# Retention, heads 1 to 7: the latent tokens' projections by seven block products; y and gate in DRAM, four weight slots

## The chip, the cores and the metric

The kernel runs on one core of a Trainium2 chip. The metric is the device time of one execution in microseconds (us). Engines are named as in the profile: PE (TensorE, with its weight loads PEld), DVE (VectorE), ACT (ScalarE), POOL (GpSimd), SP (SyncE, which here only issues DMAs).

## The reference, cut to what matters

Two layers work on 512 latent tokens and 256 context tokens of width 1024, in float32. Layer 0 is neighbourhood attention beside spatial gating, layer 1 is retention; each is followed by a gated MLP with a convolution over neighbouring tokens (FFN). The change lies in layer 1:

```python
splits = [RET_QK_WIDTH, 2 * RET_QK_WIDTH, 2 * RET_QK_WIDTH + RET_V_WIDTH]   # 1024, 2048, 4096
q, k, v, g = jnp.split(h_lat @ w_in, splits, axis=-1)
q = apply_rope(q.reshape(B, T, H, dk), cos, sin)                            # H = 8, dk = 128
k = apply_rope(k.reshape(B, T, H, dk) * dk ** -0.5, cos, sin)
v = v.reshape(B, T, H, dv)                                                  # dv = 256
kc, vc = jnp.split(h_ctx @ w_in[:, RET_QK_WIDTH:2 * RET_QK_WIDTH + RET_V_WIDTH], [RET_QK_WIDTH], axis=-1)
...
for d in range(2):                                                          # forward, backward
    s_ctx = retention_final_state(rev(kc), rev(vc), lg)
    outs_lat.append(rev(retention_chunked(rev(q), rev(k), rev(v), lg, s_ctx)))
...
on = ((o - mu) * lax.rsqrt(var + EPS)).reshape(B, N, RET_V_WIDTH) * gn_g
return (jax.nn.silu(g) * on.astype(g.dtype)) @ w_out
```

The latent tokens need all four projections, the context tokens k and v only.

## The kernel before

**Numbers.** A float32 product is made of three matmuls of a rounded type. `split` makes a high part on ACT (L171) and the rest on DVE (L172); `mm3` (L215 to L218) issues high by high, high by low, low by high. The normalized, modulated tokens lie in SBUF as such a pair (`h0c`, `h1c`).

**Weights.** A unit is 128x1024 numbers. SP loads it into one of three buffers `raw` (L157), `split` writes it into a slot of the ring `w0` to `w5`, and PE reads it there. A slot is written anew when PE has used it, a buffer when both halves of the split (and whoever else reads it) are done.

**Heads.** `retention` runs eight heads. For a head from 1 on: k (`rk`) and q (`rq`) of the latent tokens, 24 matmuls of 512 columns each; rotation (`rope`, with a product on POOL, L1221); k in natural order (`kn`); v of 128 latent tokens at a time, two to a bank, and of the context tokens, and the gate, 256 columns each (`rn`, by `nat`); scores (`rs`), states (`stc`, `stl`), the products within a chunk (`ro`) and across chunks (`rx`), and the norm with the gate (`norm`, its power on POOL, L1367). The decay matrices come from ACT and POOL (L1212, L1213). Between them stands the output product of the head before (`wr`, by `out_group`): eight pieces of 128x512, which DVE adds to y in SBUF (L678). The row of the second layer's modulation is worked out beside it on DVE (`ada_half`, `acc`, L326, six background jobs). Head 0 has an order of its own and isn't changed; the last two heads' output comes in `out_last`.

**Order.** `queue` reads the table `ORDER` and chains every engine's instructions in the order written there, one list for PE, DVE, ACT, POOL and SP each. Nothing is reordered at run time: an instruction waits at the head of its queue, and all behind it wait with it.

**The FFN.** It already uses seven products of half blocks instead of eight (`px`, `py`, `pz`), with its weight sums on DVE, and adds its result to DRAM with accumulating DMAs, issued by POOL (L1734).

Of the kernel before, what the change touches and what calls it, by code (L numbers as in the profile page):

```python
# [10 lines left out]
F32 = mybir.dt.float32  # L11
F32R = mybir.dt.float32r
# [6 lines left out]
P = 128  # L19
# [32 lines left out]
c-p;Nd8{4RS^wtDnSI~x+<kxd?Yp1-{1(SsV#izD_}N+P#Ez4YCUKi4X_Is#ZBx`#Ep3Bn)0P4)sBEQz3Mx<wv>*_mB2>|Tsf0u&{s0Li{@`D}Gt  # L52
0d*cX6Ie%CYaAJ2Pj_obxTe@ArK(PX+)BbckC8n$bRh-#=2s?*@MGjDZ{0)zEWi_4p&YxNS9|21<GeE+yMdm<kKg;1FHHn!XWj=Hk6ia<||U96SM
gxYLERfTJ7&IFfcwwyOXOU;~&_5D$0i9{3c8+s|=Hk3Z)=&Xp_pLvwKOD!l9C9CZ5Er(4@Nyawbd{;D0^#BUOh4HuzeorTj$U$$VJ3^)O9%~&$Y^
gXs$hPS_|L;JJrYh^;`yOQmM^SCNW9Q?+14X)#N6+eglLBE61YPGFbfBsdF$BbhR9n7t}kjjg-dHg&EkH$N9N6SGWUKlfGyVIYPv63!T!*4Nj-{F
h0^JqlNc&nDZ;x!Il=d#i}GSvAIfCuv$Xk{&SzipDXu1`4rKWtK8CAnkg4*o)Rsx;no6MM+EEr1tcbD}YAvF(XeX7@v&$ZUr6R4qD!>ph2?U+18J
oBE^h?c}z-ak`$vB|Q9&PqQv3mYD&$*Wq*>fawyZ``woEv$%$z$0HPo&TJgIy{;Zb3sPgTFSB(y41P{#JEHS5aELB=Z}vnav-s}pg0oO(mKLA80q
|Y!J6!ILpC|FO5O*R$9ecKaYBR5RCZvzDi$4G#W`eqf=vRf8Q33#al-=|V4l#%!%0tN|XP9#&R&@D=;l=Jns9HoYdkWwtJb8QLm6O@vc9AJ(*d!0
+_I^7usKHWk>G0od_dhszlPwu%59|Nf@9-s(S@aX>O0oSu+kS%^Bb58|CcO?{WW9cceQ5~MQDdHr-hVU^-=zpPN1gVavHjuLPJ9`=3mf9uxAf_ZS
YSDsAHa4Tt|9@)&~!HO%IdM$Vg7-G&kp>}Pe%DZ2mi_?qg5m4u_~z-e33KZZ#npD4!)OmVVAx1RJ8cv`LH|7O!u|-JRcn#Mb)Fn;vwcL^RZ(?iS0  # L60
+T(zOV7!W@zhd)M|jxR350iLo`)2k0;xS%Pu6nrUvV1j8LYHIJ&SL^3^*&;)(#5ZR-+!d=+f&I8m--%L$vXTmJ*hT||XrVZMkaPW7@P|v_;2X^|k
{?A|Ih6gwoeLpZ^_?g6#(uVBet}k<MaJv)wA5B;Z{Cq-VATmBtijaCSodQk>H*8wB(kq`FiWLVMj8LtypHF9DV$h12aIijz#Wlu~97wc0A78N%Ay
cC5Z2Wz4oYr2Cr20lywx8qP|1YuZ{yr<h!^4+e0cOZ{Y+6zRc+j_=6a9JTA?x^dN~3bqDGp*Cz<0Rsa&&O+tGHV#{^?*g-{w|NXRghvt(*BB1t-Y
# [12 lines left out]
GEf5pL<xW%Xn3#`<dOlP*Ami`$x-f4co-3iXc-w*BY68rz)Qy+v^3UA$O*i3ekz?jKQSXdd99WWrAwo)c|=IqJa@X`;%M9y$q_O=)C2|e9C&hnqV
w^~SC`DCTuTmk7V+K=OY|HS13(6t;<j^ge6e!@MUsm1N9O^AeFkMH(nu3sfM2>+k$0*wuDDK@c}B6H7|5cUVL_ndm0_*wOiZF`bqJqvG(ihfp6E-
`cIw&`4c6?=p7b|#l`DsaFU;N!-DJBWNqYc+>XGGezmTpa989%v{uu_$<NU!rs4>WFFE%=zsPxxPYKq?r`)o{FB-jSt6}YEGXiXQ6Es@+IIAB0H$
QUws%Ce_#o$*SI0oJ)A?yZ*j@<Nr30Cvd2K*<<gs0``&bYNIv-^S>yXSUcK=#{Q3l!E5+@^N$XA~4gW?K-1Po)HuK)B<2?a`$L?bwJ`u@G?s@)KI
QEQsj+LwSAdcYye1=PLyp_{yCyl;?h%QGjP|!SX+<bg_nAG87zs-#}Mla7f^Vnm>b>4Sndv1<NM$BQn%2M9q$CA7L4VTM0?j8ladvb*HFpOuxQ|Y  # L80
3vWh+@9<GwXM{B%oM_hVll80=q4$wqUe$cS1v38!o)|Bxsep*(P@d52^SYHHwP)9J`hM1=ZuzpA)5NPN%atueOJ|H>@m>tx7)5&^2(uvL$?42Hzv
`I+SjmFY>1dB=zM0o&J;sUePhlpB=C;6KxytE2QFX7MYvwB+&J;M8x#N4^<V(vT{?6tkL@R1CA31>~Hok*E5R<iFm(=`VBeCda<z^ZCRl70bz3u_
WQ(?@nvL&B$oZoQ-J_!<onNmf28pdCST8=&+cwY0U#e$ai)`jPWwh4LKAm=Kg!OTC|dY?H3q<9v8t7R=kngUi5y*_qY|jzj8v1MYYQ;ovAwZ>dUW
lNvieo1QW?(%F4SY1l-|Aq7TC5VS7yBYh@pmn@k)Ha*?C|#z0b-Kb{}GGc=hkwoJ@X{w?nP&(Y?0xsfaOV0gAG`G++(;^$o~${x>xNwR=PpNv5|G
s1~sv6Q}&z3*$>ZEG|yPoQ{}zQirKG1U(!{WdU;`K*ovoJpoAmwiTY<18}<hSq(kyca%{1?{U@idl=%aA$&nygYJb^vV44SW1AHo=v3|Cl$$W*Sg
93X{Qt84%6u7^b<@soA7n^U8kmTEts&UsHy~XYG!uLk=muT!xWF0f_(fE6@1H-KJ-XSl?)e%KCPk!-+0Uh@5WWB0E(t+s$DB6IL47(q^IH>T@;kf
MPqYTqf7JE64Wd8#hF!C>hW}4?CJdS3aq!mmn`s!rU$Y}7+lo~RuL4HS9HUaM8Z@2XSqBMONfLY+-3c6(`r+8NM=m9;0Ztr6;_2L2B?B$6NMf-PD
# [51 lines left out]
class Trunk:  # L139
# [986 lines left out]
    def weigh(self, h, b, pr, hd):  # L1126
# [46 lines left out]
    def retention(self, y, final):  # L1173
# [872 lines left out]
```

## Time and profile before

| | |
|---|---|
| median of 3 runs | 1786.44 us (1785.87 to 1786.53) |
| the profiled execution | 1785.76 us, span 1784.0 us, mean granted clock of PE 0.997 |
| layer 0 | 0 to about 390 us |
| first FFN | about 390 to 900 us |
| retention | about 905 to 1410 us |
| second FFN | about 1420 to 1784 us |

The profile is one execution. Busy times of engines overlap, so they don't add up to the span; what sets the end is seen in the chain of waits and in the windows of one stage. A row of a group has its busy time, the mean of one instruction in ns, and the idle time of its engine just before.

### The profile page before, as it was taken

What the parts mean: (1) busy time and instruction counts of PE and PEld (TensorE: products, weight loads), DVE (VectorE), ACT (ScalarE), POOL (GpSimd) and SP (SyncE); (2) the same over time, 40 slices, a digit from 0 to 9 for tenths busy, and PEclk for the clock granted to TensorE, in tenths of its full rate; (3) what the DMA queues carried; (4) which work ended last, traced back from release to release, by engine and by line L of the source; (5) the groups of instructions that cost most, each with busy time, mean ns of one, the idle gap of its engine ahead of it and who ended that gap; (6) DMA issues with size and microseconds to landing.
All of it is one profiled execution on the core that took longest, in us unless ns stands there. A gap on an engine that the chain in (4) does not pass through costs nothing.

```text
span 1784.0 us, 28774 instructions
## 1 busy us (share of the span) xinstructions
PE 1748.3 (98%) x11024; PEld 1578.7 (88%) x11024; DVE 1388.2 (78%) x2363; ACT 1017.5 (57%) x1882; POOL 340.1 (19%) x462
## 2 busy tenths in 40 slices
PE   7999999999999999999999999999999999999997
PEld 4898888799998999999899998998999789999996
DVE  3887886898887787889867666666655799998887
ACT  6633567776555555655665434433444577766773
POOL 1101322230132322222221001101001200222221
PEclk9999999999999999999999999999999999999999
DMA  8345331364687877886734332332322235887764
GB/s 304 116 133 165 99 110 45 106 180 118 171 174 174 173 174 155 164 178 161 257 126 125 118 113 71 119 95 81 97 71 60 107 122 147 214 216 185 180 145 130
DMA packets 84398, 253.44 MB, mean 142 GB/s; under 512 B 11026, under 2 KB 11538, under 8 KB 84260
## 3 DMA queue, kind: packets, MB, share of 16 engines
q1 hardware_dynamic: 55044, 191.27, 33.7%
q0 software_dynamic: 26912, 51.95, 17.1%
q10 hardware_dynamic: 2304, 8.39, 1.2%
q8 instruction: 86, 1.41, 0.3%
q14 instruction: 52, 0.43, 0.1%
HBM read 191.80 MB, written 39.85 MB: 130 GB/s over the span
## 4 chain that ended last, share of the span: by engine, by line
PE 89%; DVE 5%; ACT 3%; DMA 1%; issue 1%; POOL 1%; SPq 0%; DVEq 0%; POOLq 0%; ACTq 0%
PE px L215 11%; PE wf L216 4%; PE wf L217 4%; PE wf L218 4%; PE rn L217 4%; PE rn L216 4%; PE rn L218 4%; PE py L215 4%; PE px L216 2%; PE px L217 2%; PE px L218 2%; PE py L218 1%; PE py L217 1%; PE py L216 1%; PE ug L216 1%; PE ug L217 1%
## 5 line engine op out<-in xcount | busy, mean ns | idle before, releaser
L326 DVE SCALAR_TENSOR_TENSOR acc<-ar,cs,acc 128x512 f32<-128x512 f32 x256 | 190.5, 758 | 11.1 <-DMA ar<-in_adaw 4.3
L216 PE MATMUL rn<-rwv,h0c 128*128 128x256 f32 x384 | 107.8, 281 | 0.0
L217 PE MATMUL rn<-rwv,h0c 128*128 128x256 f32 x384 | 107.5, 281 | 0.0
L218 PE MATMUL rn<-rwv,h1c 128*128 128x256 f32 x384 | 107.2, 280 | 0.0
L1734 POOL DMA_DIRECT2D yf<-yp x64 | 56.0, 963 | 265.1 <-ACT yp L1730 237.7
L1574 ACT ACTIVATE pre<-px 128x256 f32<-128x256 f32 (+2 forms) x160 | 56.0, 369 | 78.0 <-PE px L215 55.9
L1587 DVE SCALAR_TENSOR_TENSOR cv<-pre,cw,cv 128x769 f32<-128x769 f32 (+1 forms) x88 | 77.3, 882 | 27.5 <-ACT cv L1586 26.9
L1586 ACT ACTIVATE cv<-pre,cw 128x770 f32<-128x770 f32 (+1 forms) x88 | 80.9, 925 | 21.5 <-DVE g L172 11.4
L1730 ACT COPY yp<-wf 128x512 f32<-128x512 f32 x118 | 68.4, 584 | 41.8 <-PE wf L218 34.2
L215 PE MATMUL px<-blk,wb 128*128 128x384 f32 (+1 forms) x480 | 79.2, 309 | 1.1 <-ACT pre L1574 1.1
L215 PE MATMUL px<-hs,wc 128*128 128x384 f32 (+1 forms) x480 | 78.9, 309 | 1.0 <-ACT pre L1574 0.8
L1590 DVE SCALAR_TENSOR_TENSOR cv<-pre,cw,cv 128x769 f32<-128x769 f32 (+1 forms) x88 | 76.8, 881 | 0.9
L215 PEld LDWEIGHTS px<-hs,wc 128*128 128x128 f32 x480 | 73.5, 188 | 4.1 <-ACT pre L1574 1.6
L215 PEld LDWEIGHTS px<-blk,wb 128*128 128x128 f32 x480 | 72.8, 188 | 3.8 <-ACT pre L1574 1.6
L171 ACT ACTIVATE wc<-q 128x512 fp32r<-128x512 f32 x80 | 49.8, 629 | 44.1 <-PE py L215 20.7
L216 PEld LDWEIGHTS rn<-rwv,h0c 128*128 128x128 f32 x384 | 72.4, 189 | 1.2 <-issue 0.2
L218 PEld LDWEIGHTS rn<-rwv,h1c 128*128 128x128 f32 x384 | 72.5, 189 | 0.7
L217 PEld LDWEIGHTS rn<-rwv,h0c 128*128 128x128 f32 x384 | 72.4, 188 | 0.9
L1734 POOL DMA_DIRECT2D yd<-ypg x48 | 48.4, 1053 | 122.1 <-ACT ypg L1730 104.6
L218 PE MATMUL rn<-rwg,h1c 128*128 128x256 f32 x256 | 71.3, 279 | 0.0
L217 PE MATMUL rn<-rwg,h0c 128*128 128x256 f32 x256 | 71.1, 279 | 0.0
L216 PE MATMUL rn<-rwg,h0c 128*128 128x256 f32 x256 | 71.1, 279 | 0.0
(1545 smaller groups left out, 6328.4 us busy)
## 6 DMA issues: line engine op xcount, KB each, us to landing
ar<-in_adaw SPq DMA_DIRECT2D x96, 512.0 KB
yf<-yp POOLq DMA_DIRECT2D x64, 256.0 KB, 4.3
yd<-yp POOLq DMA_DIRECT2D x54, 256.0 KB, 5.5
yd<-ypg POOLq DMA_DIRECT2D x54, 256.0 KB, 5.5
fin<-xd SPq DMA_DIRECT2D x8, 512.0 KB
xn<-in_x SPq DMA_DIRECT2D x6, 512.0 KB
xb<-in_x SPq DMA_DIRECT2D x6, 512.0 KB
xd<-xb ACTq DMA_DIRECT2D x6, 512.0 KB
```

The lines of the kernel that those rows point to most:

```text
L171: self.S.activation(hi, src, AF.Copy)
L215: mm = lambda *p, **k: self.T.matmul(*p, skip_group_check=True, **k)
L216: mm(out, lhs[0], rhs[0], start=first, stop=False)
L217: mm(out, lhs[0], rhs[1], start=False, stop=False)
L218: mm(out, lhs[1], rhs[0], start=False, stop=last)
L326: V.scalar_tensor_tensor(out=acc[s], in0=raw[:, kk * 512 : kk * 512 + 512], scalar=self.cs[:, 8 * s + k : 8 * s + k + 1], in1=acc[s], op0= ...
L1574: S.activation(pre[:, i, c : c + w], ps[:, b : b + w], AF.Copy, scale=scale)
L1586: S.activation(d, s, AF.Identity, scale=w1, bias=b)
L1587: V.scalar_tensor_tensor(out=d[:, 1:W], in0=s[:, 0 : W - 1], scalar=w0, in1=d[:, 1:W], op0=ALU.mult, op1=ALU.add)
L1590: V.scalar_tensor_tensor(out=d[:, 0 : W - 1], in0=s[:, 1:W], scalar=w2, in1=d[:, 0 : W - 1], op0=ALU.mult, op1=ALU.add)
L1730: S.copy(v, ps)
L1734: G.dma_start((yd[t] if first else y[t])[:, o], v, accum_op=ALU.add)
```

## The change

**Seven products.** With the tokens as blocks 11, 21, 12, 22 (halves of the width by halves of the tokens) and the weights of two projections stacked as blocks (k over q; v beside gate), `seven` makes seven products of half size where eight stood, into three banks X, Y, Z; X and Y take several products on top of one another (`onto`), and ACT and DVE copy, add and subtract the banks between them into float32 tiles (`kf`, `qf`; `vf`, the gate). k and q of a head: 84 matmuls of 256 columns instead of 48 of 512. v and gate: 168 of 256 instead of 192. The context tokens' k and v stay as they were.

**Sums.** The token sums are made once, on POOL (`token_sums`, nine additions of 128x1024, four splits), behind head 0. The weight sums are made in every head, on POOL: four of 128x512 (`qk_sums`), four of 128x1024 (`vg_units`). The split units of a head, output weights included, go from 8 to 13, and the gate's second unit is loaded twice.

**Room.** The weight ring has four slots (`w0` to `w3`) instead of six. y no longer lies in SBUF: ACT copies a piece into one of two tiles `yp`, and a DMA issued by POOL adds it to DRAM (`out_dram`). The gate row of the layer goes to DRAM too. After head 7, five loads of 512 KB bring y and that row back. The score tiles `sd0`, `sd1` become one; head 7 uses other tiles for its output weights.

```diff
-            rp = self.phase(ctx, "retp", 3, SLOT)
+            rp = self.phase(ctx, "retp", 1, SLOT)
...
+            def seven(name, d, shape, X, C):
+
+                x, y, z = (self.ps(f"{n}{name}", t, shape) for n, t in (("rX", "A"), ("rY", "A"), ("rZ", "C")))
+                V_ = V.tensor_tensor
+                block(x, d(11), 11, "only")
+                S.copy(C[0][0], x)
+                yield
+                block(y, d("s2"), ("t", 1), "only")
+                S.copy(C[1][1], y)
+                block(x, d("q3"), ("t", 2), "onto")
+                S.activation(C[0][1], x, AF.Copy, scale=-1.0)
+                yield
+                block(z, d(12), 21, "only")
+                V_(out=C[0][0], in0=C[0][0], in1=z, op=ALU.add)
+                block(y, d("q4"), 22, "onto")
+                V_(out=C[0][1], in0=C[0][1], in1=y, op=ALU.add)
+                yield
+                block(x, d("s3"), ("t", 3), "onto")
+                V_(out=C[1][1], in0=C[1][1], in1=x, op=ALU.subtract)
+                block(x, d(22), ("t", 4), "onto")
+                X(C[1][0], x)
+                yield
...
+                v0 = self.raw_unit(src(0, 0), f"rv0{h}")
+                put(11, v0)
+                g0 = self.raw_unit(src(16, 0), f"rg0{h}")
+                g1 = self.raw_unit(src(16, 1), f"rg1{h}")
+                t = self.bp.tile([P, 1024], F32, name=f"vt{h}", tag="G0", bufs=1)
+                sub(t, g0, g1)
+                yield d
+                v1 = self.raw_unit(src(0, 1), f"rv1{h}")
+                put(12, v1)
+                yield d
+                put("s2", t)
+                sub(g0, v0, g0)
+                sub(t, t, v0)
+                put("q3", t)
+                yield d
+                G.tensor_tensor(out=t, in0=t, in1=v1, op=ALU.add)
+                put("q4", t)
...
-                        self.out_group(f, w_out(h - 1), y, toks, h == 1, None, f"r{h - 1}")
+                        out_dram(h - 1, f, w_out(h - 1))
...
+                        v = rp.tile([P, 512], F32, name=f"yp{h}{t}{n}", tag="yp", bufs=2)
+                        S.copy(v, ps)
+                        if h == 0:
+                            G.dma_start(yd[t][:, o], v)
+                        else:
+                            G.dma_start(yd[t][:, o], v, accum_op=ALU.add)
...
+            for t in toks:
+                y[t] = self.ytile(t, "yr")
+                self.load(y[t], yd[t])
```

The table `ORDER` is a new one. Outside the retention the order is nearly as it was.

On POOL, this is the stretch of head 2 before, from its rotation (`swk`, `swq`) over a background job (`acc`) and the norm (`rrr`) to head 3's rotation:

```order
L1221 TENSOR_TENSOR swk2_10509<-swk2_10509,sin_9093 128x512
L1221 TENSOR_TENSOR swq2_10572<-swq2_10572,sin_9093 128x512
L317 MEMSET acc160_10590 128x512
L1364 TENSOR_SCALAR rrr2_11125<-rmv2_11124 128x2
L1367 TENSOR_TENSOR rrr2_11125<-rrr2_11125,mhalf_107 128x2
L1364 TENSOR_SCALAR rrr2_11125<-rmv2_11124 128x2
L1367 TENSOR_TENSOR rrr2_11125<-rrr2_11125,mhalf_107 128x2
L1221 TENSOR_TENSOR swk3_11185<-swk3_11185,sin_9093 128x512
```

The same stretch now, after head 2's rotation and the first accumulating DMA, to its last sum (`yr` from `yp`: accumulating DMAs of head 1's output; `vt2`, `rg02r`: sums of v and gate weights; `e02`: decay; `g3`: the gate row to DRAM):

```order
L1445 DMA yr0_9099<-yp101_10773 128x512
L1445 DMA yr1_9100<-yp110_10783 128x512
L1445 DMA yr1_9100<-yp111_10793 128x512
L1445 DMA yr2_9101<-yp120_10803 128x512
L1445 DMA yr2_9101<-yp121_10813 128x512
L1515 TENSOR_TENSOR vt2_10867<-rg02r_10863,rg12r_10865 128x1024
L1222 TENSOR_TENSOR e02_10606<-e02_10606,e12_10608 128x384
L1223 TENSOR_TENSOR e02_10606<-e02_10606,ident_95 128x128
L1515 TENSOR_TENSOR rg02r_10863<-rv02r_10858,rg02r_10863 128x1024
L1515 TENSOR_TENSOR vt2_10867<-vt2_10867,rv02r_10858 128x1024
L360 DMA g3_9052<-ngr150_10735 128x512
L1565 TENSOR_TENSOR vt2_10867<-vt2_10867,rv12r_10898 128x1024
```

Five accumulating DMAs, and the first one ahead of these rows, stand before the first sum `vt2`; the decay, which stood ahead of the rotation, now stands between the sums.

On PE, these rows of head 2 before lie in its value products (`rn22` of the context tokens, `rn20` of the first 256 latent tokens) and the output product of head 1 (`wr`):

```order
L217 MATMUL rn22_10703<-rwv21_10700,h0c_8691 128x256
L218 MATMUL rn22_10703<-rwv21_10700,h1c_8692 128x256
L216 MATMUL rn20_10754<-rwv20_10695,h0c_8691 128x256
L217 MATMUL rn20_10754<-rwv20_10695,h0c_8691 128x256
L218 MATMUL rn20_10754<-rwv20_10695,h1c_8692 128x256
L216 MATMUL wr121_10647<-rwo10_10599,gt01_10529 128x512
L217 MATMUL wr121_10647<-rwo10_10599,gt01_10529 128x512
L218 MATMUL wr121_10647<-rwo10_10599,gt11_10530 128x512
L348 MATMUL ag150_10584<-al150_10581,ones_101 128x512
L216 MATMUL rn22_10703<-rwv21_10700,h0c_8691 128x256
```

Now, at the place where the last score of the stretch (`rs21`) ends and the products with s2 (bank `rYv2`), 12 (`rZv2` and, for the context tokens, `rn22`) and q3 (`rXv2`) meet:

```order
L221 MATMUL rs21_11085<-rq12_10709,rk02_10706 128x256
L222 MATMUL rs21_11085<-rq02_10708,rk12_10707 128x256
L220 MATMUL rZv2_10872<-wvg212_10900,h0c_8691 128x256
L219 MATMUL rYv2_10871<-wvg2s2_10954,ht0_9685 128x256 x2
L219 MATMUL rYv2_10871<-wvg2s2_10954,ht1_9686 128x256
L219 MATMUL rXv2_10870<-wvg2q3_10959,ht2_9687 128x256
L220 MATMUL rn22_10903<-wvg212_10900,h0c_8691 128x256
L221 MATMUL rn22_10903<-wvg212_10900,h0c_8691 128x256
```

Before, the rows read two units of value weights (`rwv20`, `rwv21`) and the output weights. Now three different split units (`wvg2s2`, `wvg212`, `wvg2q3`) are read within a few rows, and the first matmul of 12 and of q3 stands ahead of the block of `rn22`.

More of the change, by code (lines that the diff above doesn't have):

```diff
@@ L1194, in retention, with k_unit @@
             w8 = lambda w: [x.rearrange("p (k c) -> p k c", k=4) for x in w]
-            qk = lambda h, o, n: self.unit(a["ret_qk"][(o + h) * P : (o + h + 1) * P], f"rw{n}{h}")
+            def k_unit(h):
+                raw = self.raw_unit(a["ret_qk"][(8 + h) * P : (9 + h) * P], f"rwk{h}")
+                u = self.slot(f"rwk{h}")
+                self.split(*u, raw)
+                return u, raw
             vg1 = lambda h, o, n, i, dst=None: w8(
@@ new lines, in block @@
+            def block(ps, w, b, kind):
+                nt = 2 if len(ps.shape) == 3 else 1
+                for i in range(nt):
+                    for k in range(4):
+                        if nt == 2:
+                            c = slice(i * P, (i + 1) * P)
+                            ops = ps[:, i, :], [x[:, k, c] for x in blk[b]], [x[:, k, :] for x in w]
+                        else:
+                            ops = ps, [x[:, k, :] for x in w], [x[:, k, :] for x in blk[b]]
+                        self.mm3(*ops, k == 0 and i == 0 and kind == "only", k == 3, kind == "onto" or i == 1)
@@ L1466, in retention @@
+                    next(run)
+                    v = hd[h]["v"]
+                    self.split(v[0][:, 0:4], v[1][:, 0:4], vf[:, 0:4])
+                    score(h, 1)
+                    next(units)
                     states(h)
-                    for tp in range(2):
-                        nat(h, wg, tp, "g")
+                    next(run)
+                    S.activation(g[:, 2:4], g[:, 2:4], AF.Silu)
                     self.bg()
                 if h < 7:
-                    wk = qk(h + 1, 8, "k")
+                    wk, rk = k_unit(h + 1)
@@ L1472, in retention @@
                 else:
-                    self.turn += 3
                     o6 = f, w_out(6)
```

312 lines of the change are left out of this document (209 added, 103 removed).

## The prediction

> **What bounds the kernel now.** I read the page first: shares of the span, then the chain that ended last.
>
> ```profile
> PE 1748.3 (98%) x11024; PEld 1578.7 (88%) x11024; DVE 1388.2 (78%) x2363; ACT 1017.5 (57%) x1882; POOL 340.1 (19%) x462
> PE 89%; DVE 5%; ACT 3%; DMA 1%; issue 1%; POOL 1%; SPq 0%; DVEq 0%; POOLq 0%; ACTq 0%
> ```
>
> TensorE is busy 98% of the span and makes 89% of the chain. An average can hide a stage, so I cut the retention and what follows it into windows.
>
> ```profile
> core 0: us, PE busy (x) PEld busy (x) DVE busy (x) ACT busy (x) POOL busy (x), PEclk, DMA share, GB/s
> 1050.00:1110.00 60.00, 60.00 (x421) 55.65 (x420) 39.77 (x69) 23.81 (x35) 7.39 (x9) 1.00 0.30 97
> 1400.00:1460.00 60.00, 54.96 (x361) 49.71 (x359) 52.69 (x91) 43.69 (x95) 10.59 (x17) 0.94 0.34 116
> 1460.00:1784.00 324.00, 313.27 (x2162) 289.92 (x2162) 285.30 (x444) 212.34 (x387) 63.66 (x76) 0.99 0.67 173
> ```
>
> Inside a head (first row) PE has no gap; DVE is at 66%, ACT at 40%, POOL at 12%. The second FFN (last row) already uses seven products and runs DVE at 88% with PE at 97%: seven products can feed PE well here. There, however, the sums of weights stand on DVE, where one takes 0.69 us:
>
> ```profile
> 1548.43 0.69 DVE L1619 TENSOR_TENSOR s<-f109r,f119r 128x512 f32<-128x512 f32 x1
> ```
>
> **The change: TensorE's work.** The answer for `rk` in two windows gives the first k matmul of head 1 and of head 7; pieces of the chain give the pitch of matmuls that follow each other.
>
> ```profile
> L216 PE MATMUL rk<-h0c,rwk x2: 395/396/396, 954.7 to 955.4; 128*128 128x512 f32 x2
> L216 PE MATMUL rk<-h0c,rwk x3: 389/395/396, 1345.3 to 1346.7; 128*128 128x512 f32 x3
> 1084.28 0.23 PE rk L216
> 1520.34 1.42 PE px L215 x12
> ```
>
> A head lasts (1345.3 − 954.7) / 6 = 65.1 us. A 512-column matmul occupies 0.23 us; a 256-column one 1.42 / 12 = 0.118 us, so half the columns cost half, to 3%. k and q go from 48 matmuls at 0.23 (11.04 us) to 84 at 0.118 (9.91), v and gate from 192 to 168 at 0.118 (22.66 to 19.82). That is 3.97 less per head, 27.8 us over seven heads, all of it on the path, since PE has no gap. A head could then last 61.1 us.
>
> **The feeders.** By the program's own counts over the whole kernel, DVE gets 38 more 128x1024 splits and 21 more 128x256 additions and loses 24 operations of 128x512 (the additions to y go; five splits a head and the combinations come). ACT gets 38 splits, 54 copies of 128x512 and 28 small operations. POOL gets 37 sums of 128x1024, 28 of 128x512 and 50 DMA issues. The rows that price them:
>
> ```profile
> L172 DVE TENSOR_TENSOR rwk<-rwk3r,rwk 128x1024 fp32r<-128x1024 f32 x1 | 1.2, 1227 | 0.0
> L678 DVE TENSOR_TENSOR yr<-wr,yr 128x512 f32<-128x512 f32 x40 | 27.2, 686 | 32.6 <-PE wr L218 32.6
> L1321 DVE TENSOR_TENSOR sd<-rs,e 128x256 f32<-128x256 f32 x32 | 12.8, 416 | 11.9 <-PE rs L218 11.9
> 947.73 1.05 ACT L171 ACTIVATE rwk<-rwk1r 128x1024 fp32r<-128x1024 f32 x1
> L1336 ACT COPY of<-ro 128x512 f32<-128x512 f32 x16 | 9.4, 585 | 9.5 <-PE ro L218 9.4
> L1221 POOL TENSOR_TENSOR swk<-swk,sin 128x512 f32<-128x512 f32 x8 | 10.4, 1300 | 29.7 <-ACT swk L1219 29.7
> L1212 POOL TENSOR_TENSOR e<-e,e 128x384 f32<-128x384 f32 x8 | 9.7, 1217 | 29.9 <-DVE m1k L1220 23.0 <-ACT e L1209 6.9
> L1213 POOL TENSOR_TENSOR e<-e,ident 128x128 f32<-128x128 f32 x8 | 4.0, 502 | 0.5
> L1734 POOL DMA_DIRECT2D yf<-yp x64 | 56.0, 963 | 265.1 <-ACT yp L1730 237.7
> yf<-yp POOLq DMA_DIRECT2D x64, 256.0 KB, 4.3
> yd<-yp POOLq DMA_DIRECT2D x54, 256.0 KB, 5.5
> ```
>
> DVE: (38 × 1.23 + 21 × 0.42 − 24 × 0.69) / 7 = 5.6 us more per head; 66% of 65.1 is 43.2, so 48.8 of 61.1. ACT: 40% of 65.1 is 26; (38 × 1.05 + 54 × 0.585) / 7 = 10.2 more, 36 of 61.1, the small ones left out. A 128x1024 sum on POOL isn't in the trace: twice the 128x512 row is 2.6, the far end if a fixed part is paid once is 2.0 (128x128 takes 0.50, 128x512 1.30: 0.27 us per 128 columns, 2.4 by that line); I take 2.6, range 2.0 to 2.6. A head then has four sums of each width (15.6 us), rope and decay as now (4.3), eight DMA issues (7.7): about 28 of 61.1, 20 of it element by element. By totals no engine binds. The Trainium skill (GPSIMD Engine Reference, § 3.1) measures a two-input fp32 addition of 2048 columns at 4497 ns on GpSimd and 2293 on VectorE, and keeps "use DVE for elementwise" as the rule; by an estimate of half its figure, 2.25, the waits below would shrink by some 2 us in all, and no row here shows a sum that wide.
>
> **The waits that appear.** Weights now pass through four slots, and a slot is free only when PE has used what it held. I follow heads 2 and 3 from the first output matmul of the preceding head's result (`wr`, time 0). A piece is six matmuls (1.38), its copy 0.585 on ACT, the accumulating DMA 0.96 to issue and 4.3 to land, with two `yp` buffers. Copies end at 2.0, 3.4, 6.9, 8.3, 11.8 and 13.2, so the sixth DMA is issued at 13.2 to 14.2. The sum `vt` = g0 − g1 (weight block s2) is queued behind it on POOL: 14.2 to 16.8. Then the split of s2 (ACT 1.05, DVE 1.23): 17.9 and 19.1. On POOL meanwhile in head 2 the decay (1.2 + 0.5) and gate − v (2.6) until 21.1, then the q3 sum, `vt` − v0, until 23.7; its high part is there at 24.8. PE's rows bring q3's first matmul at 20.1, so it is 4.7 late. The load of the second value unit (block 12) waits for the first `vt` alone, since that frees g1's buffer, and loads now take:
>
> ```profile
> 953.44 0.33 SPq L157 DMA_DIRECT2D rwo01r<-in_ret_out  x1
> 957.03 1.06 ACT L171 ACTIVATE rwo<-rwo01r 128x1024 fp32r<-128x1024 f32 x1 [0.75 <-DMA rwo01r<-in_ret_out]
> 961.37 0.33 SPq L157 DMA_DIRECT2D rwv10r<-in_ret_vg  x1
> 965.75 1.06 ACT L171 ACTIVATE rwv<-rwv10r 128x1024 fp32r<-128x1024 f32 x1 [0.84 <-DMA rwv10r<-in_ret_vg]
> ```
>
> 3.6 to 4.4 us, so it is split at 22.3 and PE wants it at about 22.5: just covered. In head 3 ACT has q3 ahead of it in its order: q3 at 23.6, the value unit at 24.7, PE wants it at 20.0, 4.7 late again. In head 1 two DMAs fewer stand there, and I take 3.0. In heads 4 to 7 POOL has `vt` ahead of most accumulating DMAs, and no such wait comes out; in 4 and 6 the DMA behind two sums delays the seventh piece by about 1.0 each. Sum 3.0 + 4.7 + 4.7 + 1.0 + 1.0 = 14.4; bounds 0 (ACT, DVE and POOL run ahead) and 7 × 4.7 = 33.
>
> **POOL and DVE at one time.** Both are in the trace side by side:
>
> ```profile
> 931.90 1.30 POOL L1221 TENSOR_TENSOR swk<-swk,sin 128x512 f32<-128x512 f32 x1
> 931.98 1.77 DVE L1222 TENSOR_TENSOR m1q<-m1q,swq 128x512 f32<-128x512 f32 x1 [0.68 <-POOL swq L1221]
> 933.68 0.68 DVE L1222 TENSOR_TENSOR m1k<-m1k,swk 128x512 f32<-128x512 f32 x1
> 971.56 1.02 POOL L1212 TENSOR_TENSOR e<-e,e 128x384 f32<-128x384 f32 x1 [0.88 <-ACT e L1209]
> 971.93 1.19 DVE L1222 TENSOR_TENSOR m1q<-m1q,swq 128x512 f32<-128x512 f32 x1
> ```
>
> (The rows are of two places, POOL and DVE each.) An addition of two SBUF tiles takes 0.68 alone, but 1.77 and 1.19 when it starts inside a POOL operation: it ends 0.5 us after POOL does, as though it had not begun before. Splits and weight sums are of this kind; additions from PSUM are not hit (`yr<-wr,yr` has 0.686 over 40). On the chain of heads 1 to 3 the split of s2 meets such a sum: 0 to 2.6 each, I take the 1.0 between the two rows' 0.5 and 1.1, together 3.0.
>
> **Start and end.** The token sums (nine of 2.6 on POOL) lie beside head 0, where POOL is mostly idle; without that cover they would cost their last link, 3 us; I take 0. At the end five loads of 512 KB more stand on SP's queue, behind the last accumulation, ahead of the last output groups; y is wanted after head 7's scores and norm. 0 to 4, I take 1.0.
>
> **The sum**, against the profiled execution's 1785.76 (0.7 below the median of the runs): −27.8 + 14.4 + 3.0 + 1.0 = −9.4, so 1776.4; I say 1776.
>
> **Rivals.** *The waits are covered.* ACT, DVE and POOL have idle time in every head, and the order table may bring the sums before PE asks. For: the last window, 97% of PE beside 88% of DVE. Against: in heads 2 and 3 the sums stand behind the sixth DMA in POOL's order, whatever the load. Then −27.8 + 1.0: 1759.
>
> *DVE becomes the bound, through POOL (slower).* Place: every head, where 20 us of POOL's sums lie beside some 30 two-input DVE operations. If a DVE operation waits in line for most of POOL's time, DVE needs 48.8 + 18 = 66.8 a head, 1.7 above today's 65.1: +12, 1798. It decides from 16.3 us of waiting per head on. For: both rows above. Against: at random, 30 operations × 20/61 (the chance to meet POOL) × 0.9 us (the rest of a POOL operation, half its length weighted by length) is 9 us, inside the 12.3 that DVE has free. The Trainium skill (SBUF — State Buffer, § Who interferes with whom) has this as its rule: a DVE instruction with two SBUF inputs and a GpSimd instruction that reads SBUF lock each other out for the whole instruction, and whoever starts first holds. The two places agree with it; it would also make POOL wait, which no row here shows.
>
> *The waits eat the gain.* If all seven heads wait as 2 and 3 do: −27.8 + 33 + 3 + 1 = +9, 1795; half way there from the forecast lies 1786, no change. For: the chain of POOL, ACT, DVE and SP is the same in each head. Against: POOL's order has `vt` early in 4 to 7.
>
> **How the numbers follow.** A measurement of this kernel can tell about 0.2% (3.6 us) from no change: 1782.9 to 1790.0 is the same. Forecast (1766 to 1783) 0.48, waits covered 0.24, gain eaten 0.14 (0.10 the same, 0.04 slower), DVE as the bound 0.14. The range reaches from the first rival to just under the second's price, 1757 to 1796, leaving out the ends of both. Faster 0.72, same 0.10, slower 0.18.
>
> **What would show it.** Right: the head period falls to about 63 in heads 2 and 3 and 61.5 in 4 to 7; PE's idle time before `rXv`, `rYv`, `rn` is released by ACT's splits; `L176` on 128x1024 has a mean above 1.23, and POOL's sums take 2.4 to 2.6. Wrong: gaps in the q and k products, a DVE above 93% of a head, gaps of more than 4.1 us in every head (slower), or no gap at all (1759).

## The result and the profile after

The changed kernel takes 1830.35 us (median of 6 runs, 1824.38 to 1840.55), the kernel before beside it 1786.06 (6 runs): ratio 1.0251, 95% interval 1.0223 to 1.0279. It is 44.3 us slower; the forecast was 9.4 us faster and the range ended at 1796. The six executions scatter over 16 us, and the mean granted clock goes with it: 0.994 in the shortest, 0.989 to 0.991 in the four around 1830, 0.984 in the longest.

First the page of the changed kernel, its busy shares and its chain by engine:

```profile
PE 1750.7 (96%) x11108; PEld 1582.1 (87%) x11108; DVE 1484.7 (81%) x2397; ACT 1097.9 (60%) x2005; POOL 525.8 (29%) x578
PE 29%; DVE 5%; POOL 5%; issue 4%; ACT 2%; DMA 1%; POOLq 0%; DVEq 0%; ACTq 0%
```

PE made 89% of the chain before. The shares of the second row add up to 46% only: the chain can be followed back no further than 974 us. Of that part PE has 29 of the 46, about 63%, and DVE, POOL and "issue" share most of the rest. Over the whole span no engine but PE is near full. The period of a head is read from the first matmul of the first k product, in head 1 and in head 7:

```profile
969.98 0.28 PE L220 MATMUL rXq<-h0c,rwk 128*128 128x256 f32 x1
1386.84 0.28 PE L220 MATMUL rXq<-h0c,rwk 128*128 128x256 f32 x1
```

(1386.84 − 969.98) / 6 = 69.5 us, against 65.1 before. Now two windows of the changed kernel and then the same two of the kernel before (columns as in the prediction). In the changed kernel the first is head 0 and the second heads 1 to 6 with most of head 7; in the kernel before the second reaches from head 1 to the beginning of the second FFN.

```profile
905.00:970.00 65.00, 56.25 (x431) 54.67 (x430) 59.82 (x68) 31.86 (x52) 40.80 (x20) 0.92 0.28 85
970.00:1440.00 470.00, 434.51 (x3147) 404.62 (x3146) 347.18 (x513) 259.92 (x394) 196.28 (x162) 0.99 0.49 125
```
```profile
905.00:970.00 65.00, 64.92 (x489) 61.62 (x488) 45.41 (x80) 38.62 (x61) 8.73 (x10) 1.00 0.38 113
970.00:1440.00 470.00, 465.97 (x3233) 430.14 (x3231) 308.70 (x547) 205.13 (x331) 58.27 (x78) 0.99 0.32 99
```

PE had next to no gap (its 4 us in the second window lie mostly behind the retention). Now it idles 8.75 us in head 0 and 35.5 in the second window, while DVE is at 92% in head 0 and at 74% in the second window. From the starts of PE's matmuls I split the whole retention, up to the same matmul of what follows it (905 to 1475 before, to 1520 after). The columns at the pitch (the time from one start to the next) of a matmul that waits for nothing make 537.0 us before, 508.0 after; gaps over 0.25 us 13.3 and 69.3; the rest (a longer pitch, a lower clock) 19.6 and 37.6. The saving in columns is there, some 29 us, and the other two take 74. (A window counts a matmul's modelled tail as busy, so it shows less of the gaps. A few records are missing, so these sums are good to about 3 us.) The largest waits of PE there:

```profile
PE rXv L221 <- DVE wvg L176: 6.6, 5, 2.1
PE rs L220 <- ACT yp L1441: 4.5, 2, 3.4
PE kn L1263 <- DVE m1k L1232: 4.0, 2, 3.4
PE wr L220 <- ACT yp L1441: 3.8, 5, 1.6
PE rYv L220 <- DVE kd L1267: 3.0, 1, 3.0
```

(Sum, times, longest.) Three of the five are released by DVE, and `m1k` and `kd` are no part of the seven products. The two rows of `yp` copies are taken up further down.

**Why DVE is late.** The timeline of head 0: POOL's token sums, then DVE, then the matmul that waited.

```profile
913.02 2.91 POOL L1459 TENSOR_TENSOR tsum<-h0c 128x1024 f32<-128x1024 f32 x1 [8.07 <-ACT h0c L175]
916.00 6.01 POOL L1459 TENSOR_TENSOR tsum<-tsum,h1c 128x1024 f32<-128x1024 f32 x2
```
```profile
912.97 3.50 DVE L176 TENSOR_TENSOR h1c<-hc,h0c 128x512 fp32r<-128x512 f32 x2
916.40 3.37 DVE L176 TENSOR_TENSOR wx<-rwq0r,wx 128x1024 fp32r<-128x1024 f32 x1
```
```profile
919.83 0.39 PE L222 MATMUL rq<-h0c,wx 128*128 128x256 f32 x1 [2.78 <-DVE wx L176]
```

A split of this size takes 1.23 us alone; `wx`, beside sums that run from 916.00 to 922.01, takes 3.37. Heads 1 to 7 show it too, here in head 2, again POOL, then DVE:

```profile
1074.39 3.36 POOL L1515 TENSOR_TENSOR rg02r<-rv02r,rg02r 128x1024 f32<-128x1024 f32 x1
1077.71 2.40 POOL L1515 TENSOR_TENSOR vt<-vt,rv02r 128x1024 f32<-128x1024 f32 x1
```
```profile
1074.08 1.44 DVE L176 TENSOR_TENSOR wvg2s<-vt,wvg2s 128x1024 fp32r<-128x1024 f32 x1 [9.96 <-ACT wvg2s L175]
1077.72 3.47 DVE L176 TENSOR_TENSOR wvg<-rv12r,wvg 128x1024 fp32r<-128x1024 f32 x1 [2.20 <-ACT wvg L175]
```

At 1077.7 POOL begins 0.01 us ahead, runs its undisturbed 2.40, and DVE ends 1.08 behind it: 2.40 + 1.07. At 1074.4 DVE is ahead, and POOL is the one that takes 3.36. This is the rule that the prediction quoted from the Trainium skill (SBUF — State Buffer, § Who interferes with whom), and the half of it that no row had shown: POOL waits too. Taking each instruction against the median of its form, DVE's lengthening is 21.0 us in head 0 and 44.9 in the 470 us behind it (6.7 per head), POOL's 4.5 and 15.8 (not all of POOL's is in the sums: some 11.5 of the 15.8); before, DVE's was 1.1 and 3.5.

**What a stall costs beside itself.** Two more windows of the changed kernel, at the stall before 919.83:

```profile
915.00:920.00 5.00, 2.22 (x19) 2.01 (x19) 5.00 (x3) 2.14 (x4) 4.84 (x3) 1.00 0.00 0
920.00:925.00 5.00, 5.00 (x31) 5.00 (x32) 4.89 (x6) 2.92 (x4) 2.51 (x2) 0.66 0.40 105
```

After a 2.8 us wait the granted clock is 0.66 over 5 us, and PE makes 31 matmuls where a free window holds 45. The Trainium skill (TensorE: Matmul & The Clock Gate, Part 1) has the clock halved after an idle window of about 3.4 us, until 3.4 us were busy: half the clock for 3.4 of 5 us is 0.66, as measured, though here 2.8 us of waiting brought it on. By such windows it happens at five places in heads 0 to 4, and costs about 10 us in all. The mean granted clock of the two profiled executions, 0.991 against 0.997, gives about the same: 0.006 of 1828 us is 11.

The traces show what decides. Their stretches at half clock last 3.41 us or twice that (apart from one at the end of each execution), and they begin at whole multiples of 3.41 from one another (in the changed kernel 17, 23, 62, 83, 101 and 181 behind its first at 863.17). Windows laid on this raster, around the wait that ends at 919.83 and around one of 3.03 us that ends at 1417.41 (PE's busy time comes first, its granted clock third from the end):

```profile
917.79:921.20 3.41, 1.37 (x11) 1.38 (x12) 3.41 (x3) 0.17 (x1) 3.33 (x2) 1.00 0.25 19
921.20:924.61 3.41, 3.41 (x18) 3.41 (x17) 3.30 (x4) 2.55 (x3) 0.92 (x2) 0.50 0.33 135
1412.72:1416.13 3.41, 1.66 (x14) 1.46 (x13) 2.79 (x3) 1.00 (x2) 1.82 (x1) 1.00 0.20 28
1416.13:1419.55 3.42, 2.14 (x18) 2.17 (x19) 3.42 (x6) 0.57 (x1) 0.00 (x0) 1.00 0.32 126
```

The shorter wait leaves PE 1.37 us busy in one interval, and half clock follows. The longer one falls on two intervals, with 1.66 and 2.14 us busy, and the clock stays. In the fourteen traces of this case, from 850 to 1520 us, half clock followed every one of the 61 full-clock intervals in which PE was busy for less than 1.57 us, and none with more than 2.11; between these, some of both.

### The profile page after: what moved, and what is told of

The parts are those of the page before. It is cut to its first block, busy times and chain, and to the rows that moved or that the text cites. A ratio compares the mean times of both kernels' runs of the same rounds, so it can differ in the third digit from the quotient of the medians.

```text
span 1828.4 us, 29401 instructions
## 1 busy us (share of the span) xinstructions
PE 1750.7 (96%) x11108; PEld 1582.1 (87%) x11108; DVE 1484.7 (81%) x2397; ACT 1097.9 (60%) x2005; POOL 525.8 (29%) x578
## 5 line engine op out<-in xcount | busy, mean ns | idle before, releaser
L330 DVE SCALAR_TENSOR_TENSOR acc<-ar,cs,acc 128x512 f32<-128x512 f32 x256 | 201.1, 801 | 11.5 <-DMA acc<-in_adab_row 5.2
L1924 POOL DMA_DIRECT2D yd<-yp x48 | 46.7, 1024 | 105.6 <-ACT yp L1920 104.0
L175 ACT ACTIVATE wb<-s 128x512 fp32r<-128x512 f32 x80 | 49.7, 629 | 31.5 <-DVE s L1809 10.4
L176 DVE TENSOR_TENSOR wb<-s,wb 128x512 fp32r<-128x512 f32 x80 | 54.6, 684 | 8.3 <-ACT wb L175 8.2
L176 DVE TENSOR_TENSOR wc<-q,wc 128x512 fp32r<-128x512 f32 x80 | 54.7, 684 | 6.3 <-ACT wc L175 6.1
L220 PE MATMUL wf<-fo,g 128*128 128x512 f32 x144 | 56.8, 394 | 0.0
L221 PE MATMUL wf<-fo,g 128*128 128x512 f32 x144 | 56.6, 394 | 0.0
L222 PE MATMUL wf<-fo,g 128*128 128x512 f32 x144 | 56.1, 391 | 0.0
L222 PE MATMUL px<-hb,wa 128*128 128x384 f32 (+1 forms) x160 | 49.4, 309 | 0.0
L221 PE MATMUL px<-hb,wa 128*128 128x384 f32 (+1 forms) x160 | 49.4, 309 | 0.0
```

Of the source, the lines that this page charges most:

```text
L175: self.S.activation(hi, src, AF.Copy)
L176: self.V.tensor_tensor(out=lo, in0=src, in1=hi.bitcast(F32), op=ALU.subtract)
L220: mm(out, lhs[0], rhs[0], start=first, stop=False)
L221: mm(out, lhs[0], rhs[1], start=False, stop=False)
L222: mm(out, lhs[1], rhs[0], start=False, stop=last)
L330: V.scalar_tensor_tensor(out=acc[s], in0=raw[:, kk * 512 : kk * 512 + 512], scalar=self.cs[:, 8 * s + k : 8 * s + k + 1], in1=acc[s], op0= ...
```

## The experiments

The theory (in the expectations P, later L): POOL's sums and DVE's two-input operations shut each other out (the lock), and that, with the clock after the stalls, is the loss. Rivals: the chain of sums, splits and loads is long because POOL is slow (W, C); the output DMAs with two `yp` buffers (R); the matmul's pitch (A, H). The kernels, with the median, and the ratio to the kernel before with its interval:

| kernel | us | ratio |
|---|---|---|
| changed | 1830.35 | 1.0251 (1.0223 to 1.0279) |
| e1: token sums away | 1818.28 | 1.0176 (1.0161 to 1.0192) |
| e2: weight sums away | 1808.27 | 1.0118 (1.0102 to 1.0133) |
| e3: both away | 1794.85 | 1.0050 (1.0035 to 1.0065) |
| e9: both away, POOL held as long | 1797.96 | 1.0067 (1.0052 to 1.0082) |
| e4: accumulating DMAs away | 1822.86 | 1.0213 (1.0188 to 1.0237) |
| e5: offsets in the slots | 1830.41 | 1.0253 (1.0238 to 1.0268) |
| e12: both sums away, offsets | 1788.37 | 1.0011 (1.0002 to 1.0021) |
| e6: all of these away | 1776.68 | 0.9947 (0.9932 to 0.9961) |
| e10: token sums on DVE | 1828.08 | 1.0238 (1.0215 to 1.0261) |
| e11: weight sums on DVE | 1812.16 | 1.0144 (1.0127 to 1.0161) |
| e7: both on DVE | 1815.04 | 1.0168 (1.0151 to 1.0185) |
| e8: both on DVE, offsets, third `yp` | 1809.85 | 1.0136 (1.0119 to 1.0153) |

**The sums taken away (e1, e2, e3).**

```diff
-                add = lambda o, x, y: G.tensor_tensor(out=o, in0=x, in1=y, op=ALU.add)
+                add = lambda o, x, y: G.memset(o, 0.37)
```
```diff
             def sub(o, x, y):
-                G.tensor_tensor(out=o, in0=x, in1=y, op=ALU.subtract)
+                G.memset(o, 0.37)
...
-                G.tensor_tensor(out=q1, in0=q0, in1=k1, op=ALU.add)
+                G.memset(q1, 0.37)
...
-                G.tensor_tensor(out=t, in0=t, in1=v1, op=ALU.add)
+                G.memset(t, 0.37)
```

The first is e1, the second e2, e3 has both.

> Leaves out the token sums: the nine 128x1024 additions on POOL become constant fills of the same tiles, which read nothing (the values are then not the sums). Theory P (POOL's sums and DVE's two-input operations shut each other out): in head 0 DVE took 21 us more than its operations take alone, PE waited 9.3 us and lost 5 us more to a lower clock, and all of that goes: about 1816 (1813 to 1820). Theory W (only the chain of weight sums, splits and loads costs time): at most 3 us, 1827 or more.

> Leaves out the weight sums of heads 1 to 7: the 56 additions on POOL become constant fills, which read nothing and take a shorter time; token sums, splits, loads, copies and accumulating DMAs stay. Theory P: DVE's 45 us of excess in these heads go, and with them most of the waits of PE for a split: about 1803 (1798 to 1810). Theory R (the two yp tiles and the accumulating DMAs are the main cost): over 1820.

> Leaves out both, token and weight sums, in the same way. Theory P: the two gains add up, about 1789 (1783 to 1796): most of the loss against the kernel before is gone, and the saving of TensorE (22 us at the pitch measured) is still eaten in part by the waits for yp and by the longer row of splits. Theory R: over 1815.

The token sums cost 12.1 us, the weight sums 22.1, both 35.5 (the three came out 2, 5 and 6 us above the expected points). But a fill is also shorter than a sum, so e3 doesn't tell the lock from POOL's slowness.

**POOL held as long, without reading (e9).** Each fill of e3 is repeated until it lasts as long as the sum.

```diff
+def long_fill(G, o):
+    wide = len(o.shape) == 3 or o.shape[1] == 1024
+    G.memset(o, 0.37)
+    G.memset(o, 0.37)
+    if wide:
+        G.memset(o[:, 0:1] if len(o.shape) == 3 else o[:, 0:256], 0.37)
```

> All token and weight sums of the changed form become constant fills on POOL, as in the kernel with both sums away (1794.9 us), but each fill is repeated on POOL until it takes as long as the sum did alone: three fills of 1.0, 1.0 and 0.3 us for a 128x1024 sum of 2.4, two of 0.57 for a 128x512 sum of 1.2. POOL is held as long as by the sums, and reads nothing. Theory L (the sums cost through locking with VectorE): 1793 to 1801 us, as without them. Rival C (the chains are late because POOL takes 2.4 us for each link, and its queue delays what else it does): 1812 us or more.

DVE's largest group in the changed kernel; then of e9 the windows, the same group, and two groups on POOL:

```profile
L330 DVE SCALAR_TENSOR_TENSOR acc<-ar,cs,acc 128x512 f32<-128x512 f32 x256 | 201.1, 801 | 11.5 <-DMA acc<-in_adab_row 5.2 <-issue 2.6 <-DMA ar<-in_adaw 2.1
```
```profile
905.00:970.00 65.00, 63.73 (x529) 62.62 (x528) 54.35 (x92) 44.14 (x71) 36.09 (x49) 1.00 0.36 109
970.00:1440.00 470.00, 448.42 (x3201) 415.31 (x3199) 337.03 (x551) 272.04 (x428) 184.32 (x257) 0.99 0.50 136
L335 DVE SCALAR_TENSOR_TENSOR acc<-ar,cs,acc 128x512 f32<-128x512 f32 x256 | 191.9, 765 | 10.4 <-DMA acc<-in_adab_row 5.4 <-issue 2.1 <-DMA ar<-in_adaw 1.4
L130 POOL MEMSET vt<- 128x1024 f32 x21 | 21.6, 1030 | 17.6 <-DVE wvg3q L181 2.4 <-DVE wvg6q L181 2.4 <-DVE wvg7q L181 2.4
L133 POOL MEMSET vt<- 128x256 f32 x21 | 6.6, 313 | 1.2
```

POOL is busy for 220 us here, in the changed kernel 237 (of which some 20 are its own lengthening). Yet PE's head 0 is almost whole, at clock 1.00, and only 3.1 of the 35.5 us are lost again. DVE's lengthening falls from 21.0 to about 3 us in head 0 and from 44.9 to about 15 behind it; the rotation and the decay on POOL still read. So most of the time was not POOL's length but what POOL's reading does to DVE, and DVE's to POOL.

One thing more goes away with the reading. A fill doesn't hold the buffers that a sum reads, so loads start sooner: that of the second value unit 25.2 us after the start of head 2 in e9, 34.6 in the changed kernel. For the weight sums e11 (below) settles it: its sums read the same buffers and that load is nearly as late (32.2), and still most of the time comes back. The token sums read no buffer that a load waits for. e9 and e11 together separate the theory from the rivals W and C.

**Accumulating DMAs (e4) and offsets (e5).** In e4 a fill of two numbers stands for each of the 40 accumulating DMAs, so the output of heads 1 to 5 isn't added.

```diff
-                            G.dma_start(yd[t][:, o], v, accum_op=ALU.add)
+                            G.memset(scr, 0.0)
```

> Leaves out the accumulating DMAs of heads 1 to 5 (40; a fill of two numbers stands in the place of each), so a yp tile is free as soon as it is written; all sums stay. Theory P: only the 8 us that PE waited for yp copies and 2 us of clock go: about 1820 (1816 to 1825). Theory R: 1805 or less.

7.5 us, and only roughly, since the two intervals overlap. It is the whole DMA that goes: the wait for a buffer, POOL's time to issue it, and the sums' wait behind it. Of the 8.3 us that PE waits for `yp` copies in the changed kernel 4.7 stay in e4, so these copies don't wait for the DMAs alone.

In e5 the units start 16 (k, q) or 48 words (v, gate) into their slot, as v and gate do in the kernel before.

```diff
-                u = self.slot(f"wvg{h}{key}")
+                u = self.slot(f"wvg{h}{key}", Q3)
...
-                wt = self.slot(f"wqt{h}")
+                wt = self.slot(f"wqt{h}", Q1)
```

> Only the place inside the weight slots changes: split v and gate units start 48 numbers (192 bytes) into their slot, as they did before the change, and k and q units 16 numbers in. In the traces the 256-column matmuls that follow each other take 0.1196 us in the changed kernel's context products against 0.1164 before, with the same tiles of tokens. Theory A (the start address of the operands sets that pitch): 0.1164 comes back in the v and gate products, seven times some 300 matmuls by 0.003, so about 7 us less, 1822 to 1825. Theory N (it comes from how the block products are queued, or from the clock): no change, 1830.

Nothing that can be told from the scatter, though the pitch of 256-column matmuls of the products fell by their starts (`rn` from 0.1196 to 0.1166 us, `rXv` on token sums from 0.1198 to 0.1149). The same is seen in one group of matmuls, of the changed kernel and of e5:

```profile
L219 PE MATMUL rXv<-wvg,ht 128*128 128x256 f32 x168 | 22.3, 283 | 0.8 <-DVE rg L1509 0.8
```
```profile
L219 PE MATMUL rXv<-wvg,ht 128*128 128x256 f32 x168 | 21.6, 279 | 0.8 <-DVE rg L1509 0.8
```

Where the gain went isn't settled. PE's gaps are 69.3 us without and 72.0 with the offsets, a difference inside the 3 us of such sums. The clock was lower too, here in the changed kernel and in e5:

```profile
905.00:1520.00 615.00, 564.20 (x4046) 524.72 (x4045) 482.59 (x712) 348.06 (x559) 253.82 (x203) 0.98 0.46 124
905.00:1524.00 619.00, 565.47 (x4058) 525.46 (x4057) 483.01 (x714) 349.59 (x562) 256.02 (x205) 0.96 0.44 123
```

PE has half clock for 27 us of the first stretch and for 44 of the second. e5's four executions had a mean granted clock of 0.985 to 0.990, the changed kernel's six 0.984 to 0.994.

**All away (e6), and the split of what that gave (e12).** e6 is e3 with e4's and e5's edits, e12 is e3 with e5's alone.

> Leaves out token sums, weight sums (constant fills) and the 40 accumulating DMAs, and has the places of e5_off: every cost that is suspected is taken away at once, the seven products, the 13 splits a head and the copies stay. If the suspects are the cause: e3_both's 1795 less 10 for the yp waits and 7 for the pitch, 1775 to 1780, under the kernel before. If the longer row of splits or the order itself is a cause of the same size: 1786 or more.

> All sums as fills (1794.9 us), and the slot units start at the offsets they had before (16 and 48 words). Without the sums and with neither the accumulating DMAs the offsets are part of a kernel at 1776.7 us, 18.1 us less; this splits those 18.1. Theory H (the pitch of 0.1196 against 0.1164 was hidden by waits in the whole changed kernel, where the offsets gave nothing; with the waits gone it counts): about 2000 block products at 0.0032 us are 6.7 us, so 1786 to 1790 us, and the accumulating DMAs have some 11. Rival (the pitch never counts, the accumulating DMAs have it all): 1794 to 1796 us.

With the waits for the sums gone, the offsets are worth 6.5 us (1794.85 to 1788.37; by the two intervals, about 4 to 10), and the accumulating DMAs the next 11.7 (to 1776.68).

**The sums on DVE (e7, e8, e10, e11).** These compute everything; the moved instructions stand in DVE's order where the trace of the changed kernel had them by time.

```diff
-                G.tensor_tensor(out=o, in0=x, in1=y, op=ALU.subtract)
+                V.tensor_tensor(out=o, in0=x, in1=y, op=ALU.subtract)
```

> Complete computation: token and weight sums on DVE instead of POOL, put into DVE's order where the trace of the changed kernel has them done on POOL; the other engines' orders stay. DVE gets some 7 us of sums a head and 10 in head 0, and loses the 6.4 and 21 that it lost to POOL. Theory P (the lock of the two engines): near e3_both, which had no sums at all, 1797 to 1806. If DVE's total work is the matter and the lock is not: 1825 or more.

> Complete computation: e7_dve with the places of e5_off and a third yp tile (room from gaps between tiles). Theory P with its smaller parts: e7_dve less 7 for the pitch and 6 for the yp waits, 1785 to 1793. If the yp waits come from POOL's late issue and not from the two tiles: 1792 to 1799.

> The changed kernel with head 0's nine token sums on VectorE, and the weight sums left on POOL. Theory L: nine sums at 1.2 us on VectorE are 11 us of a window in which VectorE has little to spare, for the 12 us that taking the sums away gave; 1820 to 1827 us. Rival: VectorE has that time free in head 0, 1816 to 1820. Had VectorE no room at all there, 1829 or more.

> The changed kernel with the 56 weight sums of heads 1 to 7 on VectorE, and the token sums left on POOL. Taking these sums away gave 22 us. Theory L: VectorE takes over 7.7 us per head, of which its shorter instructions elsewhere pay 6.4; most of the locking's price comes back, 1814 to 1820 us. Rival (what stops TensorE is VectorE's whole work per head, wherever the sums are): 1828 or more.

Of the same two windows, head 0 in e10 and the second one in e11:

```profile
905.00:970.00 65.00, 58.39 (x458) 56.83 (x456) 58.07 (x88) 36.53 (x57) 15.97 (x12) 0.95 0.31 93
```
```profile
970.00:1440.00 470.00, 446.42 (x3202) 413.50 (x3203) 375.30 (x590) 266.95 (x407) 96.89 (x117) 0.99 0.50 132
```

The weight sums on DVE give back 18.2 of their 22.1 us: DVE has room in those heads (375 of 470). At 1812.2 us e11 came out a little under the 1814 to 1820 expected. The token sums on DVE give 2.3 at most, inside the scatter, and e10 lies above the 1820 to 1827 expected: DVE is at 58 to 60 of 65 in head 0 either way, and the sums themselves now fill what the lock had filled. e7 is therefore no better than e11, and lies between what the theory and its rival had expected. e8 missed its expected 1785 to 1799 by over 10: I had added the gains of offsets and a third `yp` to e7's expected time as though PE did not wait elsewhere; e5 gave nothing for the offsets either. e8 and e11, the best complete versions, aren't told apart and stay 1.4% slower than the kernel before. A version that beats it was not found; a new order of the changed work wasn't tried.

## Why the prediction was wrong, point by point

The step that failed is the price of POOL's sums to DVE: 3.0 on the chain of three heads and 0 for the token sums, where both kinds of sums cost 35.5, about 3 of it through POOL's length. Smaller terms were off as well. Going up from e6, the runs make a sum: 1776.7 + 11.7 (accumulating DMAs) + 6.5 (pitch) + 35.5 (both kinds of sums) = 1830.4. Costs that hide one another depend on that order: taken away first, the DMAs give about 7.5 and the offsets nothing that can be told from the scatter.

- **"I take 0" for the token sums: 12.1.** The prediction looked at POOL, which was idle there (8.73 of 65), and at a last link of 3 us. What they lock out is DVE, whose `wx`, `rwg` and `m1k` PE waits for in head 0. This is the step with the wrong engine in it.
- **POOL and DVE at one time, 3.0 on three heads.** The rows were read rightly, and for the one place that I counted, the split of s2 in heads 1 to 3, the size was right as well. It takes 2.40, 1.44 (row above) and 2.70 us where 1.22 is usual, together 2.9 more:

```profile
1002.43 2.40 DVE L176 TENSOR_TENSOR wvg1s<-vt,wvg1s 128x1024 fp32r<-128x1024 f32 x1 [3.37 <-ACT wvg1s L175]
1144.69 2.70 DVE L176 TENSOR_TENSOR wvg3s<-vt,wvg3s 128x1024 fp32r<-128x1024 f32 x1 [2.37 <-ACT wvg3s L175]
```

What failed is the place: nothing was counted outside that chain. A 128x1024 split that starts together with a sum loses 2.2 us (3.47 against 1.23), and the weight sums cost 22.1 over seven heads. They fell on `wvg` and `m1k`, which met a sum, and on `kd`, which at 1416.40 stood behind two operations on `m1q` of 2.7 us each where 0.7 is usual.

- **The rival "DVE becomes the bound".** Its mechanism was the right one, its test wrong: it "decides from 16.3 us of waiting per head", because DVE has 12.3 us free. Measured are 6.7 per head, below even the 9 estimated, DVE never binds over these heads (74%), and the kernel is slower all the same. A single operation that is 2 us late stops PE if PE wants it next; free time elsewhere in the head doesn't give that back. That POOL would wait too it named, and gave no price.
- **Waits of the POOL chains, 14.4.** Of this, 12.4 stood for the sixth DMA, the sum `vt` behind it and the split of s2, in heads 1 to 3. The trace has that chain, but shorter, and it stops PE at another place than the product with q3. In head 2 ACT's split waits for `vt`, two copies of `wr` stand behind the split in ACT's order, and the scores wait 3.44 us for these copies:

```profile
1070.28 2.68 POOL L1515 TENSOR_TENSOR vt<-rg02r,rg12r 128x1024 f32<-128x1024 f32 x1
1072.99 1.06 ACT L175 ACTIVATE wvg2s<-vt 128x1024 fp32r<-128x1024 f32 x1 [3.57 <-POOL vt L1515]
1073.95 1.05 ACT L1441 COPY yp<-wr 128x512 f32<-128x512 f32 x2
1074.57 0.41 PE L220 MATMUL rs<-rq,rk 128*128 128x256 f32 x1 [3.44 <-ACT yp L1441]
```

PE waits 1.05 and 0.86 us behind the same chain in head 1, 1.26 and 1.29 in head 3. That is 7.9 in all, with some of the lock in it, where 3.0 + 4.7 + 4.7 stood. Head 2's wait is 3.39 in e9, where POOL takes as long, and the same scores wait 0.92 in e11, where DVE makes the sum. So this term was right in kind and too large; it is not what made the kernel slower. POOL's sum was sized well: 2.40 alone against 2.6 taken; half the figure of the Trainium skill (GPSIMD Engine Reference, § 3.1), an estimate, is 2.25. For the wait on the two `yp` buffers I took 2.0. The accumulating DMAs cost 7.5 to 11.7, with POOL's issues and what queues behind them; how much of it is the buffers wasn't told apart. In head 2 one copy stands 3.00 us for a DMA, and PE's next piece of `wr` 1.58 behind it:

```profile
1068.83 0.58 ACT L1441 COPY yp<-wr 128x512 f32<-128x512 f32 x1 [3.00 <-DMA yr<-yp]
```

- **TensorE's work, −27.8 "all of it on the path".** The columns fell by as much, but the pitch of 0.118 came from another stage (`px`); the products ran at 0.1196 to 0.1199 as their units now start at the slot's beginning, 6.5 us once the sums are gone. And with sums, DMAs and pitch all taken away the gain is 9.4, not 27.8. The windows of e6, and its longest waits:

```profile
970.00:1440.00 470.00, 455.93 (x3360) 425.75 (x3360) 351.77 (x585) 285.88 (x458) 109.97 (x180) 0.99 0.36 120
PE wr L220 <- ACT yp L1443: 2.7, 3, 2.0
PE rXv L221 <- DVE wvg L176: 2.1, 3, 1.1
PE pf L221 <- DVE hb L176: 1.8, 2, 1.2
PE rXq L219 <- DVE fq L1511: 1.8, 3, 0.8
```

PE's starts give 511.4 columns, 26.6 gaps and 23.1 of the rest in e6. Against before that is −25.6, +13.3 and +3.5: some twenty gaps of 0.6 to 2.2 us, behind copies, additions between products and splits, hand-overs that eight full products mostly didn't have (PE's waits in the list above name them; no run takes them away one by one). That e6 came out at the forecast's 1776 is chance: it lacks all that the forecast had added.

- **The clock after a stall** was in no term; about 10 us of the 44 by the windows.
- **The end reload, 1.0:** no wait of PE at that place shows it.
- **"What would show it".** Of the signs named for wrong, "gaps of more than 4.1 us in every head" came, by PE's starts 4.4 to about 9 in each of heads 1 to 7, and so did the gaps in q's products; a DVE above 93% did not. Of those named for right, POOL's 2.4 and the longer splits (a mean of 1.38 on 128x1024 against 1.23) held, but the lock gives them as well. The head period (69.5 where 61.5 to 63 stood) did not, and PE's waits before `rXv` end with DVE's half of a split, not with ACT's.

## What to carry to other kernels

Before moving element work to an idle engine, ask whether the two shut each other out while they read, as POOL's sums and DVE's splits did here. The price isn't the mover's time but what each of the other's operations waits for, and it falls on whatever stands on the path at that moment. Compare a stall with the time until the waiting engine wants the result, not with the late engine's free time per stage. Gains of edits to a kernel with many waits need not add: remove the largest first, and price the smaller ones in what is left.

## What was not expected of the hardware

- DVE and POOL shut each other out in both directions, whole instruction by whole instruction (3.47 = 2.40 + 1.07 and 3.36 against 2.40), while fills on POOL, which read nothing, left DVE near its own pace (`acc` 765 ns against 801; 758 before). Two one-input operations were caught too: `on<-of` took 2.61 us beside POOL's decay (at 1258.23) and 2.48 beside a sum (at 1392.56) where 0.41 is usual.
- The pitch of a 256-column matmul depended on where the unit of weights starts in its slot: 0.1196 us (`rn`) at the slot's start, 0.1166 at 48 words. Why wasn't tried.
- A wait of 2.8 us of TensorE was followed by 3.4 us at half clock; waits of 2.1 (at 1276.6 and 1342.2) and one of 3.0 (at 1417.4) were not. How little PE is busy in one interval of a raster of 3.41 us decided it, so a wait's length alone doesn't tell.
